# Redistributing the eight PSUM banks of a recurrence: three for projections, two for values, outputs and norms, three shared by levels, key transposes and state increments

## The chip, the cores and the metric

The kernel runs on one core of one Trainium2 chip. The metric is the device time of one execution in microseconds (us); where several runs are shown, their median stands.

## What is computed

One trunk layer of a hybrid diffusion model over 128 context and 1024 latent tokens (1152 in all, D_MODEL 1024): a gated feed-forward half step, a token mixer, and a second feed-forward half step. The mixer projects the normalised input with `w_in` and splits the result; one part goes to attention, the other to a gated recurrence (HGRN2, 8 heads of 64, run forward and backward). The change lies in the recurrence:

```python
def hgrn2_chunked(q, k, logf, v, s0):
    ...
    A = jnp.einsum('bntshk,bnthk,bnshk->bnhts', decay, qc, kc)
    o_intra = jnp.einsum('bnhts,bnshv->bnthv', A, vc)
    g = b[:, :, -1]
    dS = jnp.einsum('bnshk,bnshv->bnhkv', kc * jnp.exp(g[:, :, None] - b), vc)
    def step(S, inp):
        gj, dSj = inp
        return jnp.exp(gj)[..., None] * S + dSj, S
    s_final, S_prev = lax.scan(step, s0.astype(jnp.float32), ...)
    o_inter = jnp.einsum('bnthk,bnhkv->bnthv', qc * jnp.exp(b), S_prev)
    return (o_intra + o_inter).reshape(B, T, H, DV), s_final
...
    q_h = jax.nn.silu(heads(hq, HG_DK))
    f_fw = lb_h[0] + (1.0 - lb_h[0]) * jax.nn.sigmoid(heads(hf_f, HG_DK))
    o_rec = rmsnorm(o_fw + flip(o_bw), hg_norm_g) * jax.nn.silu(heads(hgate, HG_DV))
```

## The kernel before

One program on one core: first feed-forward, mixer (recurrence, attention, merge), second feed-forward. Activations lie features on partitions, tokens along the free dimension. The 1152 tokens are cut into three chunks of CW = 384, worked in ORDER (2, 0, 1); the 8 heads go in 4 pairs, and a 128-partition tile holds a head's forward state in its lower and its backward state in its upper half.

**Projections.** One projection of one chunk is 8 blocks of 128 inputs, each with three float32r products (high times high L467, low times high L468, high times low L469), so 24 matmuls that add up in one PSUM bank of tag `mm`. `dense_g` yields after the first 12, so that other work of the weave can come between the halves. Readers of the bank: `proj_f` (forget gate: ACT sigmoid L664, then L676), `proj_q` (sigmoid L664, DVE multiply L687), `proj_v` (ACT copy `t` L698), `proj_gate` (sigmoid L664, DVE multiply L742, then POOL's multiply L735 with the normed output), `proj_sg` (sigmoid L664, then a DMA). Weights come by SP's queue and are split into a high part on ACT (`wh`, L230 or L240) and a low part (`wl`, DVE L233 or POOL L241).

**Recurrence.** `scan_pre` makes, of one head and chunk, the cumulated gates: `kk` (ACT L867, L868), a copy of q (L871), X and Y (ACT L877, DVE L879 to L882, POOL), then the scaled keys and queries `Kb`, `Qb`, `KE` (DVE L887 to L900). `scan_lev` takes them through the levels: matmuls of keys and queries within blocks of 8, then 16, 32, 64 tokens (`lv`, L932), each level read by DVE (copy_predicated L939, L974) or ACT (L958), with DVE's decays of KE (L969) and ACT's copies of its halves (`kr`, L944 and L945) in between; then it turns the keys (`kt`, L984, copied by ACT L986), and multiplies them with the values into the chunk's state increments (`dS`, L994, copied by ACT L995). `scan_out` runs the states (DVE L1004) and adds inter and intra parts up in PSUM (`po`), which ACT copies out (L1020). `turn_v` turns the projected values (`vt`, L705, ACT copy L706). After a pair's two heads, `proj_gate` squares the output, and its inner `norm` calls `rec_norm` for the three chunks: a matmul with ones (`ops`), then ACT and DVE (L359 to L363), then L1030. The norm before the mixer does the same with `nps` (L451, in `stat_end`), its tag given by `self.st`.

**Banks.** The PSUM pool `pp` of this stage has all 8 banks of 512 floats: `lv` 3, `sm` 3, `mm` 2 (L759 to L761). A tile takes the banks of its tag in turn, and its first matmul waits until the last reader of the bank's former tile is done. Before, `sm` holds `nps`, `vt`, `kt`, the increments (`dS`), `po` and `ops`. `attn`, which follows, has a pool of its own over the same eight banks, with three `mm` banks.

**Order.** Every engine runs its instructions in one fixed order. `hgrn` weaves projections, the current chunk's levels (`cur`), the former chunk's end (`old`), the next one's `scan_pre` (`pre`) and the outputs by hand, in groups and slots; the framework's scheduler then places each instruction when the program is built, by what it takes to be ready, and so the number of banks can move instructions on each engine. A few are pinned in program order.

Of the kernel before, what the change touches and what calls it, by code (L numbers as in the profile page):

```python
# [9 lines left out]
F32 = mybir.dt.float32  # L10
# [9 lines left out]
P = 128  # L20
# [6 lines left out]
CW = 384  # L27
# [3 lines left out]
ORDER = (2, 0, 1)  # L31
# [57 lines left out]
class Trunk:  # L89
# [550 lines left out]
    def mixer(self):  # L640
        nc, tc = self.nc, self.tc
        dram = lambda n, sh: self.dp.tile(sh, F32, name=n)
        self.sg = dram("sgates", [2, KT, P, T])
        self.orec = dram("orec", [4, P, T])
        self.oat = dram("oat", [4, P, T])
        with ExitStack() as st:
            self.fp = st.enter_context(tc.tile_pool(name="hp", bufs=1, reuse_waits="tile"))
            self.pp = st.enter_context(tc.tile_pool(name="pp", bufs=1, space=PSUM, reuse_waits="tile"))
            self.st, self.nt, self.hfb = ("sm", 3), ("t", 3), 2
            self.hgrn()  # L650
        with ExitStack() as st:
            self.kp = self.fp = st.enter_context(tc.tile_pool(name="kp", bufs=1, reuse_waits="tile"))
            self.pp = st.enter_context(tc.tile_pool(name="pp", bufs=1, space=PSUM, reuse_waits="tile"))
            self.attn()
# [45 lines left out]
            yield  # L700

    def turn_v(self, out, c, t):
        pt = self.pp.tile([P, CW], F32, tag="sm", bufs=3, name="vt")
        for j in range(3):
            self.nc.tensor.transpose(pt[:, ts(j, P)], t[:, ts(j, P)], self.ident)  # L705
        self.nc.scalar.copy(out["V"][:, c * CW : (c + 1) * CW], pt)  # L706
        out["nv"] = out.get("nv", 0) + 1
# [48 lines left out]

    def hgrn(self):
        nc, pin = self.nc, self.tc.keep_in_program_order
        self.mmb = 2  # L759
        for tag, n in (("lv", 3), ("sm", 3), ("mm", 2)):  # L760
            self.pp.tile([P, 512], F32, tag=tag, bufs=n, name=tag)  # L761
        f32 = lambda n, sh: self.fp.tile(sh, F32, name=n)
        A, B = slice(0, 64), slice(64, P)
        self.kr = {m: f32(f"kr{m}", [P, CW]) for m in (8, 16, 32, 64)}
        self.XY = [f32(n, [P, 48, 8]) for n in "XY"]
        self.A1 = [f32(f"A1_{i}", [P, 3, G]) for i in range(2)]
        self.A2 = f32("A2", [P, 3, G])
        self.cnt, self.later = 0, []
        heads = [{} for _ in range(H)]
        pairs = [{} for _ in range(4)]  # L770
        sgs = [self.proj_sg(j) for j in range(2 * KT)]

        def feed(h):
            p = h // 2
            r = [self.proj_f(5 * p + h % 2, h, heads[h])]
            if h % 2 == 0:
                r += [self.proj_q(5 * p + 2, pairs[p]), self.proj_v(5 * p + 3, pairs[p])]
            return r

        def scan_of(h):  # L780
            p = h // 2
            if h % 2 == 0:
                pairs[p]["o"] = self.tt(F32, "oT")
            d = heads[h]
            d["pair"] = pairs[p]
            d["h"], d["QP"], d["As"] = h, self.tt(F32, "QP"), {}
            d["Gall"] = self.fp.tile([P, 9], F32, tag="Gall", bufs=2, name="Gall")
            return d

        def work_of(h):  # L790
            p = h // 2
            work = feed(h + 1) if h + 1 < H else []
            if h and h % 2 == 0:
                work = work + [sgs.pop(), sgs.pop()] + [self.proj_gate(5 * p - 1, p - 1, pairs[p - 1])]
            while len(work) < 4 - (h == 3) + (h == H - 1):
                work.append(sgs.pop())
            return chain(*work)

        pre = iter(())
        for i, _ in enumerate(weave(feed(0))):  # L800
            if i < 12:
                next(self.tail, None)
            if i == 11:
                assert next(self.tail, 1)
                for t in self.XY:
                    pin(nc.vector.memset(t[:, :, 3:4], 1.0))
                d = scan_of(0)
                pre = self.scan_pre(d, ORDER[0])
            if i == 13:
                for t in self.A1 + [self.A2] + list(self.kr.values()):  # L810
                    pin(nc.vector.memset(t, 0.0))
            next(pre, None)
        for _ in pre:
            pass
        self.group()
        work = chain.from_iterable(map(work_of, range(H)))
        old = cur = out = last = None
        for p in range(H * NCH + 1):
            h, n = divmod(p, NCH)
            old, cur, pre = cur, None, iter(())  # L820
            if h < H:
                cur = self.scan_lev(d, ORDER[n])
            if p + 1 < H * NCH:
                h1, n1 = divmod(p + 1, NCH)
                while min(heads[h1].get("nf", 0), pairs[h1 // 2].get("nq", 0)) <= n1:
                    next(work)
                if n1 == 0:
                    last, d = d, scan_of(h1)
                pre = self.scan_pre(d, ORDER[n1])

            def slots(k):
                for _ in range(k):
                    next(work, None)
                    next(pre, None)

            self.group(old, cur)
            slots(3)
            self.group(old, cur, old, out)
            slots(2 + p % 2)
            self.group(cur, out, old)  # L840
            out = None
            if p and n == 0:
                out = self.scan_out(last if h < H else d)
                next(out)
            slots(2)
            for _ in pre:
                pass
        self.group(out, out)
        for _ in work:
            pass  # L850
        for n, _ in enumerate(self.proj_gate(19, 3, pairs[3])):
            if n == 0:
                self.group()
# [51 lines left out]
    def scan_lev(self, d, b):  # L905
# [10 lines left out]
        dS = d["dS"]  # L916
# [6 lines left out]
        lv = lambda: self.pp.tile([P, 3, 64], F32, tag="lv", bufs=3, name="lv")  # L923
# [25 lines left out]
        for li, m in enumerate((8, 16, 32, 64)):  # L949
# [29 lines left out]
                    nc.scalar.copy(Af[u, :, u], Ad[u])  # L979
            Tm = Tn  # L980
            yield
        pt = self.pp.tile([P, 3, P], F32, tag="sm", bufs=3, name="kt")
        for j in range(3):
            nc.tensor.transpose(pt[:, j], KE[:, ts(j, P)], self.ident)  # L984
        kT = tmp("kT", 2, (P, 3, P))
# [1 line left out]
        yield  # L987
        V = d["pair"]["V"]
        assert d["pair"]["nv"] > ORDER.index(b)
        pd = self.pp.tile([P, 3, 64], F32, tag="sm", bufs=3, name="dS")  # L990
        for j in range(3):
            for r in (A, B):
                v = V[:, (3 * b + j) * P + 64 * hh : (3 * b + j) * P + 64 * hh + 64]
# [3 lines left out]
    def scan_out(self, d):  # L997
        nc = self.nc
        h, V, QP, Gall, S, dS = d["h"], d["pair"]["V"], d["QP"], d["Gall"], d["S"], d["dS"]
        A, B = slice(0, 64), slice(64, P)  # L1000
        nc.sync.dma_start(self.o["st"][h], dS[:, 8])
        for j in range(7):
            for r, s0, s1, g in ((A, j, j + 1, j), (B, 7 - j, 6 - j, 7 - j)):
                nc.vector.scalar_tensor_tensor(S[r, s1], S[r, s0], Gall[r, g : g + 1], dS[r, g], ALU.mult, ALU.add)  # L1004
        yield
        off = 64 * (h % 2)
        r = slice(off, off + 64)
        for pairs, lows, highs in (((3, 4), (2, 5)), (2, 4), (4, 6)), (((1, 6), (0, 7), (8,)), (0, 2), (6, 9)):
            po = self.pp.tile([P, 3, P], F32, tag="sm", bufs=3, name="po")
            at = lambda t: po[A, t - lows[0]] if t < lows[1] else po[B, t - highs[0]]  # L1010
            for pair in pairs:
                for t in pair:
                    w = V[:, t * P + off : t * P + off + 64]
                    nc.tensor.matmul(at(t), w, d["As"][t // 3][:, t % 3], start=True, stop=(t == 8))
                for t in pair:
                    if t < 8:
                        nc.tensor.matmul(at(t), S[:, t], QP[:, ts(t, P)], start=False, stop=True)
            for half, (t0, t1) in ((A, lows), (B, highs)):
                pv = po[half, : t1 - t0].rearrange("p a b -> p (a b)")
                nc.scalar.copy(d["pair"]["o"][r, t0 * P : t1 * P], pv)  # L1020
            d["pair"]["no"] = d["pair"].get("no", 0) + 1
            yield

    def rec_norm(self, c, oT, sq):
        nc = self.nc
        cs = slice(c * CW, (c + 1) * CW)
        ps = self.pp.tile([P, CW], F32, tag="sm", bufs=3, name="ops")
        nc.tensor.matmul(ps, self.onesb, sq[:, cs], start=True, stop=True)
        self.rstd(sq[:, cs], ps)
        nc.vector.scalar_tensor_tensor(oT[:, cs], oT[:, cs], self.hg, sq[:, cs], ALU.mult, ALU.mult)  # L1030
# [873 lines left out]
```

## Time and profile before

| what | value |
|---|---|
| median of 3 runs | 2897.6 us (2895.7 to 2897.98) |
| profiled execution, its own time | 2896.19 us |
| its span | 2894.2 us |
| mean granted TensorE clock | 0.989 |
| instructions in the span | 54329 |

The span runs from the first to the last recorded instruction; the 2 us around it belong to the execution's time. Engines: PE is TensorE's matmuls, PEld its weight loads, DVE VectorE, ACT ScalarE, POOL GpSimd, SP the engine that issues DMAs. In a timeline row stand start, duration, engine, source line, operation, result and operands, shape, and in brackets the idle time of the engine just ahead of it with what released it. The recurrence stretches from about 838 us (its norm `nps`) to 1431 us, where attention's first projection starts.

### The profile page before, as it was taken

How to read it: one execution, taken by the hardware profiler on the slowest of the kernel's cores; microseconds unless marked ns; L12 is line 12 of the kernel's file. 1: busy time of each engine (PE TensorE's matmuls, PEld its weight loads, DVE VectorE, ACT ScalarE, POOL GpSimd, SP SyncE). 2: the span in 40 equal slices, each digit the busy share in tenths (PEclk: the TensorE clock that was granted, in tenths of full speed). 3: DMA queues.
4: the chain of work that ended last, by engine and by line, in shares of the span. 5: the costliest groups of instructions: out<-in, count | busy, mean ns of one | idle time of the engine just before them, and what ended most of it. 6: DMA issues, size and time to landing. Idle time of an engine off the chain costs nothing. (4 is left out here: it accounts for less than half of the span.)

```text
span 2894.2 us, 54329 instructions
## 1 busy us (share of the span) xinstructions
PE 2803.6 (97%) x20946; PEld 2665.0 (92%) x20946; DVE 1967.4 (68%) x4292; ACT 1278.4 (44%) x2566; POOL 943.4 (33%) x896
## 2 busy tenths in 40 slices
PE   6999999999999999999998999899999999999998
PEld 5999999999999988888987777699999999999997
DVE  7687777577778787876266777856756665556665
ACT  6433222321166677766446777711642323333102
POOL 0133332454222222222145454433333232236321
PEclk9999999999999999999998999999999999999999
DMA  6643333653121111112100001333442322235211
GB/s 240 212 146 119 131 116 122 234 192 117 56 74 65 45 56 39 56 46 74 68 17 17 13 16 49 100 126 101 166 133 95 105 83 77 73 134 186 91 46 66
DMA packets 151490, 282.43 MB, mean 98 GB/s; under 512 B 19200, under 2 KB 83776, under 8 KB 151232
## 3 DMA queue, kind: packets, MB, share of 16 engines
q1 hardware_dynamic: 151232, 278.96, 28.0%
q8 instruction: 165, 2.70, 0.4%
q14 instruction: 93, 0.76, 0.1%
HBM read 215.37 MB, written 63.52 MB: 96 GB/s over the span
## 5 line engine op out<-in xcount | busy, mean ns | idle before, releaser
L1652 PE MATMUL b<-xo,wo 128*128 128x288 f32 x3552 | 482.4, 295 | 0.0
L1652 PEld LDWEIGHTS b<-xo,wo 128*128 128x128 f32 x3552 | 474.5, 188 | 0.0
L496 DVE SCALAR_TENSOR_TENSOR x<-dn,modt,x 128x256 f32<-128x256 f32 (+4 forms) x728 | 353.4, 505 | 168.8 <-PE dn L469 166.2
L1652 PE MATMUL b<-bh,wo 128*128 128x288 f32 x1776 | 365.9, 295 | 1.2 <-ACT et L1662 1.2
L467 PE MATMUL mm<-xh,wh 128*128 128x384 f32 (+1 forms) x1008 | 352.1, 349 | 10.8 <-DVE sg L742 6.0
L468 PE MATMUL mm<-xl,wh 128*128 128x384 f32 (+1 forms) x1008 | 342.1, 339 | 0.0
L469 PE MATMUL mm<-xh,wl 128*128 128x384 f32 (+1 forms) x1008 | 341.4, 339 | 0.0
L1652 PEld LDWEIGHTS b<-bh,wo 128*128 128x128 f32 x1776 | 289.2, 188 | 1.5 <-ACT et L1662 1.4
L1652 PE MATMUL b<-bl,wo 128*128 128x288 f32 x888 | 262.4, 295 | 0.0
L241 POOL TENSOR_TENSOR wl<-raw,wh 128x1024 fp32r<-128x1024 f32 (+3 forms) x71 | 151.3, 2133 | 273.4 <-ACT wh L240 270.7
L1627 ACT CAST wo<-raw 128x512 fp32r<-128x512 f32 x185 | 114.7, 621 | 227.6 <-PE b L1652 117.4
L467 PEld LDWEIGHTS mm<-xh,wh 128*128 128x128 f32 (+1 forms) x1008 | 189.6, 188 | 20.9 <-DVE sg L742 8.2
L467 PE MATMUL dn<-hh,wh 128*128 128x384 f32 (+2 forms) x576 | 196.7, 341 | 1.7 <-DVE et L1668 0.9
L1628 DVE TENSOR_TENSOR wo<-raw,wo 128x512 fp32r<-128x512 f32 x185 | 127.2, 688 | 103.3 <-ACT wo L1627 100.4
L469 PE MATMUL dn<-hh,wl 128*128 128x384 f32 (+2 forms) x576 | 194.4, 337 | 1.0 <-POOL wl L241 1.0
L468 PE MATMUL dn<-hl,wh 128*128 128x384 f32 (+2 forms) x576 | 194.6, 338 | 0.0
L468 PEld LDWEIGHTS mm<-xl,wh 128*128 128x128 f32 (+1 forms) x1008 | 189.4, 188 | 2.3 <-issue 0.7
L469 PEld LDWEIGHTS mm<-xh,wl 128*128 128x128 f32 (+1 forms) x1008 | 189.3, 188 | 1.0
L1730 POOL TENSOR_TENSOR hl<-hr,hh 128x1152 fp32r<-128x1152 f32 x44 | 118.0, 2689 | 193.8 <-ACT hh L1729 92.5
L312 DVE SCALAR_TENSOR_TENSOR junk<-wada,cb 128x512 bf16<-128x512 f32 x224 | 165.7, 740 | 8.5 <-DMA wada<-in_w_aT 7.8
L1384 POOL TENSOR_TENSOR ehl<-e,ehl 128x512 fp32r<-128x512 f32 x93 | 122.5, 1322 | 142.1 <-ACT ehl L1382 79.0
L1652 PEld LDWEIGHTS b<-bl,wo 128*128 128x128 f32 x888 | 167.2, 188 | 0.0
(392 smaller groups left out, 6867.8 us busy)
## 6 DMA issues: line engine op xcount, KB each, us to landing
raw<-in_w SPq DMA_DIRECT2D x148, 256.0 KB, 3.2
raw<-in_w SPq DMA_DIRECT2D x58, 512.0 KB, 3.7
wada<-in_w_aT SPq DMA_DIRECT2D x112, 256.0 KB, 2.9
hr<-hs SPq DMA_DIRECT2D x44, 576.0 KB, 5.2
hs<-et SPq DMA_DIRECT2D x148, 144.0 KB, 1.8
raw<-in_w_in SPq DMA_DIRECT2D x41, 512.0 KB, 3.2
hb<-hd SPq DMA_DIRECT2D x44, 288.0 KB, 3.4
x<-in_xT SPq DMA_DIRECT2D x16, 576.0 KB, 6.4
```

Source lines behind the costliest of these rows:

```text
L241: pin((eng or self.nc.gpsimd).tensor_sub(wl, raw, wh))
L312: nc.vector.scalar_tensor_tensor(junk, ws[n % 2], 1.0, cs[s], ALU.mult, ALU.mult, accum_out=o)
L467: pin(nc.tensor.matmul(ps, wh, xh, start=start and i == 0, stop=False))
L468: pin(nc.tensor.matmul(ps, wh, xl, start=False, stop=False))
L469: pin(nc.tensor.matmul(ps, wl, xh, start=False, stop=stop and i == n - 1))
L496: nc.vector.scalar_tensor_tensor(self.x[m][:, a:b], ps[:, a - lo : b - lo], self.modt[:, gm, m, s : s + 1], self.x[m][:, a:b], ALU.mult, A ...
L1384: eng.tensor_sub(el, e, eh)
L1627: nc.scalar.copy(wh, src[i])
L1628: nc.vector.tensor_sub(wl, src[i], wh)
L1652: nc.tensor.matmul(ps, w[:, k], x[:, k, :QW], start=first, stop=last, skip_group_check=home != i)
L1730: nc.gpsimd.tensor_sub(hl, raw, hh)
```

## The change

Eight banks stay eight. `mm` has three and `sm` two. `nps`, `kt` and the increments move from `sm` to `lv`; `vt` and `po` stay in `sm`; of the three `ops` of a pair the first two stay in `sm`, and the third takes an `mm` bank.

```diff
--- before.py
+++ after.py
@@ -646,7 +646,7 @@
         with ExitStack() as st:
             self.fp = st.enter_context(tc.tile_pool(name="hp", bufs=1, reuse_waits="tile"))
             self.pp = st.enter_context(tc.tile_pool(name="pp", bufs=1, space=PSUM, reuse_waits="tile"))
-            self.st, self.nt, self.hfb = ("sm", 3), ("t", 3), 2
+            self.st, self.nt, self.hfb = ("lv", 3), ("t", 3), 2
             self.hgrn()
         with ExitStack() as st:
             self.kp = self.fp = st.enter_context(tc.tile_pool(name="kp", bufs=1, reuse_waits="tile"))
@@ -700,7 +700,7 @@
             yield
 
     def turn_v(self, out, c, t):
-        pt = self.pp.tile([P, CW], F32, tag="sm", bufs=3, name="vt")
+        pt = self.pp.tile([P, CW], F32, tag="sm", bufs=2, name="vt")
         for j in range(3):
             self.nc.tensor.transpose(pt[:, ts(j, P)], t[:, ts(j, P)], self.ident)
         self.nc.scalar.copy(out["V"][:, c * CW : (c + 1) * CW], pt)
@@ -756,8 +756,8 @@
 
     def hgrn(self):
         nc, pin = self.nc, self.tc.keep_in_program_order
-        self.mmb = 2
-        for tag, n in (("lv", 3), ("sm", 3), ("mm", 2)):
+        self.mmb = 3
+        for tag, n in (("lv", 3), ("sm", 2), ("mm", 3)):
             self.pp.tile([P, 512], F32, tag=tag, bufs=n, name=tag)
         f32 = lambda n, sh: self.fp.tile(sh, F32, name=n)
         A, B = slice(0, 64), slice(64, P)
@@ -979,7 +979,7 @@
                     nc.scalar.copy(Af[u, :, u], Ad[u])
             Tm = Tn
             yield
-        pt = self.pp.tile([P, 3, P], F32, tag="sm", bufs=3, name="kt")
+        pt = self.pp.tile([P, 3, P], F32, tag="lv", bufs=3, name="kt")
         for j in range(3):
             nc.tensor.transpose(pt[:, j], KE[:, ts(j, P)], self.ident)
         kT = tmp("kT", 2, (P, 3, P))
@@ -987,7 +987,7 @@
         yield
         V = d["pair"]["V"]
         assert d["pair"]["nv"] > ORDER.index(b)
-        pd = self.pp.tile([P, 3, 64], F32, tag="sm", bufs=3, name="dS")
+        pd = self.pp.tile([P, 3, 64], F32, tag="lv", bufs=3, name="dS")
         for j in range(3):
             for r in (A, B):
                 v = V[:, (3 * b + j) * P + 64 * hh : (3 * b + j) * P + 64 * hh + 64]
@@ -1006,7 +1006,7 @@
         off = 64 * (h % 2)
         r = slice(off, off + 64)
         for pairs, lows, highs in (((3, 4), (2, 5)), (2, 4), (4, 6)), (((1, 6), (0, 7), (8,)), (0, 2), (6, 9)):
-            po = self.pp.tile([P, 3, P], F32, tag="sm", bufs=3, name="po")
+            po = self.pp.tile([P, 3, P], F32, tag="sm", bufs=2, name="po")
             at = lambda t: po[A, t - lows[0]] if t < lows[1] else po[B, t - highs[0]]
             for pair in pairs:
                 for t in pair:
@@ -1024,7 +1024,8 @@
     def rec_norm(self, c, oT, sq):
         nc = self.nc
         cs = slice(c * CW, (c + 1) * CW)
-        ps = self.pp.tile([P, CW], F32, tag="sm", bufs=3, name="ops")
+        tag = ("sm", 2) if ORDER.index(c) < 2 else ("mm", 3)
+        ps = self.pp.tile([P, CW], F32, tag=tag[0], bufs=tag[1], name="ops")
         nc.tensor.matmul(ps, self.onesb, sq[:, cs], start=True, stop=True)
         self.rstd(sq[:, cs], ps)
         nc.vector.scalar_tensor_tensor(oT[:, cs], oT[:, cs], self.hg, sq[:, cs], ALU.mult, ALU.mult)
```

One line is added, so lines behind L1027 have a number higher by one in the changed kernel.

In the built program the numbers of instructions and SP's order stay as they were. Orders differ on PE, DVE, ACT and POOL at the start of the recurrence only, in the stretch from about 845 to 905 us of the profile before. On PE, the third projection of each round of the first feed (f, q, v) now runs its first 12 matmuls ahead of the second halves of the other two, and the third chunk's value transposes (`vt`) stand 10 rows earlier among the level products.

On ACT, before the change, from the sigmoid of the third forget projection of head 0 (`sg_9356`) on, to the key copies of the first chunk and the first value copy. `kr32` and `kr64` are the key halves of levels 32 and 64, `kk`, `X`, `Y` belong to the `scan_pre` of head 0's third chunk, `wh` are weights of the projections to come, `t` and `V` the turned values:

```order
L664 ACTIVATE sg_9356<-mm_9282 128x384
L676 ACTIVATE fs_9035<-sg_9356,lb_86,lb1_87 64x384 x2
L867 ACTIVATE kk_9718<-fs_9035 64x384
L868 ACTIVATE kk_9718<-fs_9035 64x384
L877 COPY X_9030<-fs_9035 128x48
L877 COPY Y_9031<-fs_9035 128x48
L230 COPY wh_9629<-raw_9627 128x1024
L664 ACTIVATE sg_9382<-mm_9303 128x384
L945 COPY kr32_9028<-KE_9339 64x6x32
L944 COPY kr64_9029<-KE_9339 64x3x64
L230 COPY wh_9850<-raw_9848 128x1024
L698 COPY t_9397<-mm_9324 128x384
```

On ACT at the same place after the change:

```order
L664 ACTIVATE sg_9356<-mm_9282 128x384
L945 COPY kr32_9028<-KE_9339 64x6x32
L676 ACTIVATE fs_9035<-sg_9356,lb_86,lb1_87 64x384 x2
L664 ACTIVATE sg_9382<-mm_9303 128x384
L230 COPY wh_9629<-raw_9627 128x1024
L944 COPY kr64_9029<-KE_9339 64x3x64
L698 COPY t_9397<-mm_9324 128x384
L706 COPY V_9092<-vt_9399 128x384
L706 COPY V_9092<-vt_9404 128x384
L945 COPY kr64_9029<-KE_9339 64x3x64
L706 COPY V_9092<-vt_9409 128x384
L867 ACTIVATE kk_9718<-fs_9035 64x384
```

The key copy L945 of `kr32` now stands right behind the sigmoid and ahead of the pair L676 of the forget gate; `kk`, `X` and `Y` and the weights `wh_9850` have gone behind the value copies.

On DVE, at the same place in the program, before the change, from the second keys of head 0 (`Kb_9553`) to the state of the first chunk's keys (`KE_9339`, which L945 reads) and the third q multiply. `wl` is the low part of the weights:

```order
L887 TENSOR_TENSOR Kb_9553<-kk_9471,Y_9031 64x384
L233 TENSOR_TENSOR wl_9454<-raw_9451,wh_9453 128x512 x2
L888 TENSOR_TENSOR Qb_9554<-qx_9474,X_9030 64x384
L892 COPY TK_9573<-Y_9031 64x48
L893 COPY TK_9573<-X_9030 64x48
L894 TENSOR_TENSOR TQ_9574<-X_9030,fs_9035 64x48
L895 TENSOR_TENSOR TQ_9574<-Y_9031,fs_9035 64x48
L900 TENSOR_TENSOR KE_9555<-Kb_9553,TK_9573 128x384
L896 TENSOR_TENSOR T8_9575<-TK_9573,TQ_9574 128x48
L969 TENSOR_TENSOR KE_9339<-KE_9339,T16_9528 64x12x16
L969 TENSOR_TENSOR KE_9339<-KE_9339,T32_9596 64x6x32
L879 TENSOR_TENSOR X_9030<-fs_9035,X_9030 128x48
```

On DVE at the same place after the change:

```order
L887 TENSOR_TENSOR Kb_9553<-kk_9471,Y_9031 64x384
L888 TENSOR_TENSOR Qb_9554<-qx_9474,X_9030 64x384
L892 COPY TK_9573<-Y_9031 64x48
L893 COPY TK_9573<-X_9030 64x48
L894 TENSOR_TENSOR TQ_9574<-X_9030,fs_9035 64x48
L895 TENSOR_TENSOR TQ_9574<-Y_9031,fs_9035 64x48
L900 TENSOR_TENSOR KE_9555<-Kb_9553,TK_9573 128x384
L896 TENSOR_TENSOR T8_9575<-TK_9573,TQ_9574 128x48
L969 TENSOR_TENSOR KE_9339<-KE_9339,T16_9528 64x12x16
L969 TENSOR_TENSOR KE_9339<-KE_9339,T32_9596 64x6x32
L233 TENSOR_TENSOR wl_9454<-raw_9451,wh_9453 128x512 x2
L969 TENSOR_TENSOR KE_9339<-KE_9339,T32_9596 64x6x32
```

The pair L233 of `wl_9454` has moved from ahead of the keys' scaling to behind the L969 multiplies of `KE_9339`.

The third place is on PE near the end of the third pair, at about 1237 us of the profile before, where the order stays and only the waits differ. `mm_14459` is a forget projection, `lv_14475` a level product of the older chunk, `lv_14501` and `lv_14502` the first products of the next chunk, forward and backward half; in brackets stand the engines whose semaphores an instruction waits for. Before the change:

```order
L469 MATMUL mm_14459<-xh3_8452,wl_14455 128x384
L932 MATMUL lv_14475<-QP_13551,kr32_9028 32x32 [waits DVE_49,Pool_49]
L932 MATMUL lv_14475<-QP_13551,kr32_9028 32x32 x11
L932 MATMUL lv_14501<-Qb_14359,Kb_14358 32x32
L932 MATMUL lv_14502<-Qb_14359,Kb_14358 32x32 [waits DVE_49,PE_49]
```

After the change:

```order
L469 MATMUL mm_14459<-xh3_8452,wl_14455 128x384
L932 MATMUL lv_14475<-QP_13551,kr32_9028 32x32 [waits DVE_49,Pool_49]
L932 MATMUL lv_14475<-QP_13551,kr32_9028 32x32 x11
L932 MATMUL lv_14501<-Qb_14359,Kb_14358 32x32 [waits DVE_49,PE_49]
L932 MATMUL lv_14502<-Qb_14359,Kb_14358 32x32 [waits Activation_49]
```

The bank of `lv_14502` was last read by DVE before the change; now its last reader is ACT, whose copy L995 takes the increments of an earlier chunk out of that bank.

Behind the recurrence, attention's first projection keeps its place. Its bank was last read by the third norm's readers before, and by the L742 multiply of the last gate projection after.

## The prediction

> **What bounds the kernel now.** I read the page's engine table first, then the windows view over the recurrence (the only place the change touches), then the waits of PE there, and last single rows of the timeline.
>
> ```profile
> span 2894.2 us, 54329 instructions
> PE 2803.6 (97%) x20946; PEld 2665.0 (92%) x20946; DVE 1967.4 (68%) x4292; ACT 1278.4 (44%) x2566; POOL 943.4 (33%) x896
> ```
>
> Over the whole span PE is the bound: 2803.6 of 2894.2 us. But this share is a mean over stages. The next fence cuts the recurrence into stretches; the columns are the stretch, its length, and the busy time of PE, weight load, DVE, ACT and POOL, then the granted clock.
>
> ```profile
> 838.00:883.00 45.00, 43.01 (x265) 41.30 (x265) 36.32 (x79) 31.42 (x64) 9.69 (x15) 0.94 0.14 48
> 883.00:950.00 67.00, 67.00 (x779) 63.40 (x778) 54.20 (x151) 41.84 (x107) 15.02 (x26) 0.97 0.22 75
> 1015.00:1248.00 233.00, 223.63 (x2737) 205.82 (x2730) 189.93 (x497) 168.90 (x404) 53.66 (x91) 0.99 0.14 50
> 1337.00:1417.00 80.00, 80.00 (x823) 75.70 (x823) 27.29 (x76) 35.48 (x85) 12.93 (x15) 1.00 0.22 78
> 1431.00:1510.00 79.00, 79.00 (x445) 74.81 (x444) 40.85 (x64) 27.36 (x48) 34.47 (x29) 1.00 0.08 26
> ```
>
> In 883 to 950, 1337 to 1417 and 1431 to 1510 PE never stops: whatever delays PE there delays the end. In 1015 to 1248 it stands still for 233.00 - 223.63 = 9.4 us. What PE waits for, over the whole recurrence up to 1431 (total, times, longest):
>
> ```profile
> PE mm L467 <- DVE sg L742: 6.0, 5, 1.8
> PE mm L467 <- DVE q L687: 4.3, 3, 2.3
> PE mm L467 <- ACT sg L664: 0.4, 1, 0.4
> ```
>
> These are the waits of a projection's first matmul for a bank: 6.0 + 4.3 + 0.4 = 10.7 us, 0.37% of the time, and all that a third bank could give back.
>
> Who drives the middle stretch decides what those waits are worth. I followed the work back from the last copy below to the first row below, each time to what released an instruction or to the instruction ahead of it on its engine.
>
> ```profile
> 1015.01 0.49 ACT L664 ACTIVATE sg<-mm 128x384 f32<-128x384 f32 x1 [1.89 <-issue]
> 1247.70 0.47 ACT L698 COPY t<-mm 128x384 f32<-128x384 f32 x1
> 1248.23 0.55 PE L705 MATMUL vt<-ident,t 128*128 128x128 f32 x3 [0.65 <-ACT t L698]
> ```
>
> Between these two ACT rows lie 530 instructions end to end (330 of DVE, 191 of ACT, 9 of POOL), none of PE, with no stop but table loads and hand-overs. PE enters at 1015 and takes over again at 1248.23, where it waits 0.65 us for ACT. The two engines wait for each other inside the stretch, not for PE:
>
> ```profile
> ACT Af L979 <- DVE Ad L977: 20.6, 8, 3.8
> ACT kk L867 <- DVE Kb L887: 17.1, 8, 3.9
> ...
> DVE X L879 <- ACT X L877: 8.2, 5, 2.0
> DVE S L1004 <- ACT dS L995: 7.9, 5, 2.3
> ```
>
> So from 1015 to 1248 the length is set by the ACT and DVE chain, and PE's waits there are its slack.
>
> **The change, part by part.** Counts of instructions, SBUF addresses and DMA issues stay the same, and the order on SP too. On PE, DVE, ACT and POOL the order differs only at the start of the recurrence, about 845 to 905 us; behind it only PE's bank waits differ.
>
> *Third projection bank.* The built program no longer waits at these first matmuls:
>
> ```profile
> 849.98 0.45 PE L467 MATMUL mm<-xh,wh 128*128 128x384 f32 x1 [0.40 <-ACT sg L664]
> 1078.22 0.44 PE L467 MATMUL mm<-xh,wh 128*128 128x384 f32 x1 [0.48 <-DVE sg L742]
> 1114.72 0.44 PE L467 MATMUL mm<-xh,wh 128*128 128x384 f32 x1 [2.32 <-DVE q L687]
> 1336.76 0.44 PE L467 MATMUL mm<-xh,wh 128*128 128x384 f32 x1 [0.47 <-DVE sg L742]
> ```
>
> With the two other q L687 waits that makes 0.40 + 0.48 + 4.3 + 0.47 = 5.65 us. The three remaining waits for L742, 6.0 - 0.48 - 0.47 = 5.05 us, stay: the third norm (`ops` of the last chunk) now takes the third bank, so the next projection still stands behind the first gate's multiply. Of the 5.65 us, the 0.48 and the 4.3 lie inside the chain stretch, where I cost them at **0**; if that cover were gone they would be worth -4.78. The 0.47 at 1336.76 stands right ahead of a stretch in which PE is never idle: **-0.47**. The 0.40 belongs to the start, below.
>
> *Key transposes, increments and the first norm in the level banks.* Now a level product can meet a bank whose reader is ACT's copy of the transposes (L986) or of the increment (L995). By the rows of before, five products would come too early; these are the largest three, each with the copy that it now waits for:
>
> ```profile
> 980.10 0.62 PE L932 MATMUL lv<-Qb,Kb 64*32 64x32 f32 x48
> 980.30 0.32 ACT L995 COPY dS<-dS 128x192 f32<-128x192 f32 x1
> ...
> 1107.39 0.62 PE L932 MATMUL lv<-Qb,Kb 64*32 64x32 f32 x48
> 1107.86 0.32 ACT L995 COPY dS<-dS 128x192 f32<-128x192 f32 x1
> ...
> 1237.68 0.62 PE L932 MATMUL lv<-Qb,Kb 64*32 64x32 f32 x48
> 1238.84 0.32 ACT L995 COPY dS<-dS 128x192 f32<-128x192 f32 x1
> ```
>
> The copies end at 980.62, 1108.18 and 1239.16: waits of 0.52, 0.79 and 1.48 us, 2.79 together, and two more that are each shorter than the first, at most 1.04: 3.83 at the outside. Behind the waiting product stand, on PE, the remaining products of that level and the next projection half; DVE waits for the products, ACT's sigmoid for the projection. What hides it: at 1237.68 the next projection's bank would have come late in before, and the copy at 1247.70 reads a projection that PE finished ahead of this row:
>
> ```profile
> 1245.88 0.89 PE L932 MATMUL lv<-QP,kr 128*64 128x64 f32 x36
> ```
>
> That is a lead of 1247.70 - 1245.88 = 1.8 us against a delay of 1.48 at most, and freed q L687 waits lie between. I take **0**; the bound above is 3.83, the one below 0, since a wait added on PE frees nothing.
>
> *The start.* With three banks the third projection of a round runs its first half ahead of the first two's second halves, and ACT's and DVE's orders follow. PE does the same matmuls. What stands on the path is ACT ahead of the value transposes:
>
> ```profile
> 874.29 0.48 ACT L664 ACTIVATE sg<-mm 128x384 f32<-128x384 f32 x1
> 874.81 1.44 ACT L676 ACTIVATE fs<-sg,lb,lb 64x384 f32<-64x384 f32 x2
> ...
> 880.53 0.35 ACT L945 COPY kr<-KE 64x192 f32<-64x192 f32 x1 [1.05 <-DVE KE L969]
> 881.00 0.35 ACT L944 COPY kr<-KE 64x192 f32<-64x192 f32 x1
> 881.25 1.04 ACT L230 CAST wh<-raw 128x1024 fp32r<-128x1024 f32 x1
> 882.20 0.47 ACT L698 COPY t<-mm 128x384 f32<-128x384 f32 x1
> ...
> 875.75 1.29 DVE L233 TENSOR_TENSOR wl<-raw,wh 128x512 fp32r<-128x512 f32 x2
> 880.02 0.94 DVE L969 TENSOR_TENSOR KE<-KE,T 64x192 f32<-64x192 f32 x2
> ```
>
> The key copy L945 moves ahead of L676, directly behind the sigmoid that ends at 874.77. DVE's weight pair of 1.29 us moves behind the key multiplies, so the copy starts at 880.53 - 1.29 = 879.24; then 0.35, L676 1.44, the next sigmoid 0.48, the weight cast 1.04, a key copy 0.35: t is copied at 882.90 in place of 882.20, **+0.70**. The kk, X and Y of the chunk after (L867, L877) fall behind the value copies, by some 6 us; PE's 67.00 of 67.00 us behind 883 hides that, since it works on projections. From below, the freed 0.40 at 849.98 bounds it: -0.40. From above, see the third rival.
>
> A rule on the clock belongs beside these stalls. Behind the 2.32 us stall the trace has this:
>
> ```profile
> 1116.20:1119.60 3.40, 3.40 (x46) 2.78 (x44) 3.27 (x8) 1.80 (x3) 0.88 (x1) 0.50 0.02 5
> ```
>
> So a stall can cost a further 3.4 us at 0.50 of the clock, 1.7 us of work, and this one lies inside the chain stretch. The Trainium skill, "TensorE: Matmul & The Clock Gate", section "What's actually happening", says that the clock is halved after at least one idle window of about 3.4 us, that the window runs free and that the same kernel can meet it at another phase. The length agrees with the row; the stall here was shorter than the window, so the measurement is the stricter one. By the page the waits added here, all below 1.7 us, would halve no clock and the sum would stay as it is; by the row a halved window more or less is possible in any run.
>
> *The tail.* Attention's first projection keeps its place, but its bank is now that of the last gate's last projection:
>
> ```profile
> 1430.80 0.34 PE L467 MATMUL mm<-xh,wh 128*128 128x384 f32 x1
> 1431.92 0.56 DVE L742 TENSOR_TENSOR sg<-mm,sg 128x384 f32<-128x384 f32 x1 [1.34 <-POOL sg L735]
> ```
>
> PE started it without a wait at 1430.80; now it waits for DVE's multiply, which ends at 1432.48: **+1.68**. Behind it on PE stands all of attention's projecting, 79.00 of 79.00 us busy, so nothing hides it. A halved window behind it would add 1.7.
>
> **Sum** on the profiled execution of 2896.19 us (span 2894.2): 0 - 0.47 + 0 + 0.70 + 1.68 = +1.91. That execution lies 1.41 below the median of three, 2897.6; the same step on the median gives **2899.5 us**.
>
> **Rivals.**
>
> *A, PE is the bound after all.* For it: 97% busy. The Trainium skill, "Perfetto Trace Analysis", section "Optimization Strategy", takes a repeated gap on the engine that should be saturated as a sign of too little PSUM; by it this change is the remedy. As a mechanism of this kernel: all 5.65 us freed count, the tail's 1.68 stays, ACT's copies come earlier with PE so that the level waits cost nothing: 2897.6 - 5.65 + 1.68 = 2893.6, and 2891.9 if the halved window at 1116 goes too. Against it: the unbroken 530 steps without PE.
>
> *B, the level waits are passed on.* If PE's lead of 1.8 us before ACT is used up, the 3.83 us count: 2899.5 + 3.83 = 2903.3. It decides from a delay beyond 1.8 us; the largest here is 1.48, and a halved window of 1.7 behind it would go past that.
>
> *C, the start stalls ACT (slower).* If DVE's multiply for L945 does not come 1.29 us earlier, and the work behind it (L676, casts, sigmoid) is needed sooner than I count, ACT stands from 874.77 to 880.53, 5.76 us, and all of it reaches the transposes: 2899.5 - 0.70 + 5.76 = 2904.6. It decides once L676's result, now after 879.6 and not 874.81, is what the next stage waits for. For it: a wait put ahead of ready work in an in-order queue. Against it: ACT's 31.42 busy of 45 us leaves room to catch up.
>
> *D, the change does less than it says.* Since the third norm takes the bank, half of the removed waits stay anyway; this is in the sum already.
>
> **How the numbers follow.** Forecast 0.65 (2895.5 to 2902.5: the start's -0.40, a halved window more or less, the spread of the runs shown), A 0.14, B 0.08, C 0.13. About 0.2%, 5.8 us, is what a measurement of this kernel can tell from no change. Faster than 2891.8 needs A with the halved window and some more: 0.08, of A. Slower than 2903.4 takes C, half of B and a little of the forecast with a halved window: 0.18. The rest, 0.74, is within. The range reaches to A's lower end and C's time: 2892 to 2905.
>
> **What would show it.** Right: the first matmuls at 1114.72, 1235 and 1241 without waits, yet the copy of t before the transposes at 1248 as long after the sigmoid at 1015 as before (232.7 us); waits of PE for ACT's dS copy at about three places; a wait of 1.7 us before attention's first projection, named L742. Wrong: the distance from 1015 to 1248 shrinking by over 2 us (A), or growing by over 2 us (B), or ACT idle for over 5 us before L945 at about 875 with PE idle behind it (C). A halved window that appears in one and not in the other kernel would shift the time by 1.7 us for no reason of the change.

## The result, and the profile after

The changed kernel takes 2904.59 us (median of 9 runs, 2900.89 to 2905.91), the kernel before 2896.7 us (9 runs, 2895.1 to 2897.98): a ratio of 1.0025, 95% interval 1.0016 to 1.0034. It is slower by 7.9 us, where 1.9 us was forecast; the time lies just inside the upper end of the range (2905), 2.1 us above the band of the forecast itself (2895.5 to 2902.5).

Head of the page after:

```profile
span 2902.8 us, 54343 instructions
PE 2805.7 (97%) x20946; PEld 2669.4 (92%) x20946; DVE 1966.0 (68%) x4292; ACT 1278.5 (44%) x2566; POOL 940.7 (32%) x896
```

No engine has more work than before (PE's 2.1 us more go with a clock that is halved for 73.6 us of the span instead of 66.8): the span has grown by waits and by halved clock. The waits of PE over the recurrence of the changed kernel (total, times, longest):

```profile
PE mm L467 <- DVE sg L742: 6.6, 4, 1.8
PE vt L705 <- ACT V L706: 5.0, 1, 5.0
PE nps L451 <- DVE rs L377: 4.5, 1, 4.5
PE lv L932 <- ACT dS L995: 3.4, 3, 2.3
PE vt L705 <- ACT t L698: 2.6, 4, 1.6
PE lv L932 <- DVE QP L969: 1.9, 2, 1.6
PE lv L932 <- POOL QP L969: 1.3, 1, 1.3
PE dS L994 <- ACT kT L986: 0.8, 1, 0.8
```

The bank waits for q L687 are gone, as the change promises, and so are two of the five for L742; one for L742 is new, ahead of attention. Three rows are new: a single wait of 5.0 us of the value transposes for ACT, 3.4 us of level products for ACT's copies of the increments, and one of 1.3 us of level products for POOL.

**A ledger.** One and the same matmul (the n-th of its source line) can be looked up in two traces. The table gives, by stage, how much later than in the profile of before the matmuls start at the stage's end, less the same at its beginning; each end is the middle value of the matmuls in 1.2 us of before's time. "Ahead" is what an execution had lost before the recurrence began, which the change cannot touch. The last column but one is the sum of the five stages from 839 to 1431.

| stage (us of before) | ahead | 839-905 | 905-1015 | 1015-1249 | 1249-1337 | 1337-1431 | recurrence | 1431-2870 |
|---|---|---|---|---|---|---|---|---|
| changed kernel | 1.41 | 3.43 | 0.25 | 1.29 | 0.91 | 1.87 | 7.75 | -0.57 |
| the same again (e8) | 0.77 | 3.60 | 0.17 | 0.17 | -0.66 | 1.84 | 5.12 | 2.29 |
| e1 levels only | 1.18 | 0.04 | 0.11 | 0.08 | 0.12 | 0.03 | 0.38 | 1.61 |
| e2 start restored | 0.40 | -0.35 | 0.22 | -0.21 | -0.65 | 0.04 | -0.95 | 2.76 |
| e3 tail restored | -0.22 | 3.21 | 0.26 | 0.27 | -0.64 | -0.12 | 2.98 | 2.35 |
| e4 start and tail | 1.56 | -0.84 | 0.18 | 0.29 | -0.66 | -0.05 | -1.08 | 1.24 |
| e5 before again | -0.28 | 0.08 | 0.01 | 0.10 | 0.01 | 0.03 | 0.23 | -0.53 |

The two executions of the changed kernel agree on three entries: the start, 3.4 to 3.6 us; the last pair's freed wait and what follows, when no halved window falls there; and the tail, 1.8 us. They differ by 1.1 and 1.6 us in 1015-1249 and 1249-1337, and behind the recurrence.

**The start.** ACT's rows in the changed kernel, where the chain to the value transposes runs; then DVE's and PE's:

```profile
877.07 0.48 ACT L664 ACTIVATE sg<-mm 128x384 f32<-128x384 f32 x1
881.92 0.35 ACT L945 COPY kr<-KE 64x192 f32<-64x192 f32 x1 [4.37 <-DVE KE L969]
882.30 1.44 ACT L676 ACTIVATE fs<-sg,lb,lb 64x384 f32<-64x384 f32 x2
883.76 0.49 ACT L664 ACTIVATE sg<-mm 128x384 f32<-128x384 f32 x1
884.27 1.04 ACT L230 CAST wh<-raw 128x1024 fp32r<-128x1024 f32 x1
885.23 0.35 ACT L944 COPY kr<-KE 64x192 f32<-64x192 f32 x1
885.48 0.47 ACT L698 COPY t<-mm 128x384 f32<-128x384 f32 x1
885.85 0.85 ACT L706 COPY V<-vt 128x384 f32<-128x384 f32 x2
...
881.54 0.74 DVE L969 TENSOR_TENSOR KE<-KE,T 64x192 f32<-64x192 f32 x2
882.20 1.28 DVE L233 TENSOR_TENSOR wl<-raw,wh 128x512 fp32r<-128x512 f32 x2
...
886.37 0.90 PE L705 MATMUL vt<-ident,t 128*128 128x128 f32 x3 [4.98 <-ACT V L706]
```

ACT stands 4.37 us in front of the key copy L945, and everything behind it in its queue waits along. In before it did L676 and other work in that time, and waited 1.05 us for the same copy. Less the 1.41 us of "ahead", L945 starts at 880.51; in before it was 880.53. So it did not come earlier at all, though the weight pair L233 has indeed gone behind DVE's key multiply. The reason lies further up, from the first sigmoid of the stage on:

```profile
851.01 0.62 ACT L402 ACTIVATE xh<-xn,modt 128x384 fp32r<-128x384 f32 x1 [1.50 <-DVE xn L401]
851.65 1.28 ACT L664 ACT_TABLE_LOAD   x1
852.95 0.49 ACT L664 ACTIVATE sg<-mm 128x384 f32<-128x384 f32 x1
...
855.46 0.56 DVE L687 TENSOR_TENSOR q<-mm,sg 128x384 f32<-128x384 f32 x1 [3.17 <-ACT sg L664]
...
865.53 1.60 DVE L811 MEMSET kr<- 128x384 f32 x4
...
869.29 0.55 DVE L887 TENSOR_TENSOR Kb<-kk,X 64x384 f32<-64x384 f32 x1
```

The same rows of before:

```profile
848.14 1.28 ACT L664 ACT_TABLE_LOAD   x1
849.43 0.49 ACT L664 ACTIVATE sg<-mm 128x384 f32<-128x384 f32 x1
849.82 0.61 ACT L402 ACTIVATE xh<-xn,modt 128x384 fp32r<-128x384 f32 x1
...
852.30 0.56 DVE L687 TENSOR_TENSOR q<-mm,sg 128x384 f32<-128x384 f32 x1 [1.22 <-ACT sg L664]
...
866.32 0.55 DVE L887 TENSOR_TENSOR Kb<-kk,X 64x384 f32<-64x384 f32 x1
...
882.72 0.55 PE L705 MATMUL vt<-ident,t 128*128 128x128 f32 x3 [1.59 <-ACT t L698]
```

In the new order ACT does the fourth L402 ahead of its table load, and waits 1.50 us for DVE's norm to do it; the first sigmoid comes 852.95 - 849.43 - 1.41 = 2.1 us later. DVE waits 3.17 us for ACT's sigmoids in place of 1.22, and stands idle for 5.3 us in all between its fourth L401 and its first scaled keys, in before for 4.0; these keys come 869.29 - 866.32 - 1.41 = 1.56 us later. That eats the 1.29 us that the weight pair was to give back. The transposes start 886.37 - 882.72 - 1.41 = 2.24 us late. Some 0.4 us of this come from the two banks of values and outputs: t is copied by 885.95, but the third value tile then waits for ACT's copy L706 of the first one to free its bank, hence the name of the wait; in before it waited for t alone. The other 1.2 us of the stage lie behind the transposes, where the clock stays halved for two windows (885.6 to 892.5); before it was one (884.1 to 887.5).

**The clock.** Two stretches of 3.4 us in the changed kernel, and what follows each (columns as in the windows view: stretch, length, PE, weight load, DVE, ACT, POOL, granted clock, DMA share, GB/s):

```profile
1134.80:1138.20 3.40, 1.81 (x77) 1.17 (x76) 2.75 (x11) 3.10 (x8) 0.55 (x1) 1.00 0.02 5
1138.20:1141.60 3.40, 3.40 (x12) 3.40 (x13) 3.19 (x10) 1.88 (x7) 0.03 (x1) 0.50 0.00 0
1336.20:1339.60 3.40, 1.61 (x10) 1.38 (x9) 1.96 (x5) 3.34 (x5) 1.27 (x2) 1.00 0.02 5
1339.60:1343.00 3.40, 3.40 (x13) 3.40 (x12) 3.24 (x7) 3.30 (x8) 0.68 (x2) 0.50 0.16 58
```

And in before, ahead of its halved window at 1116, and at a stall that brought none:

```profile
1112.80:1116.20 3.40, 1.48 (x8) 1.48 (x9) 3.25 (x10) 1.03 (x2) 0.00 (x0) 1.00 0.00 0
1328.00:1331.50 3.50, 2.00 (x43) 1.40 (x42) 3.34 (x8) 3.44 (x5) 0.00 (x0) 1.00 0.00 0
```

Three of these four windows at full clock, with PE busy for 44 to 53% of them, were followed by one at 0.50; the one with 57% was not. Before, the halved window fell at 1116, inside the stretch where PE has slack, and cost nothing: e1 below has none there, and takes as long for this stretch (232.8 us against 232.7). In the first profile of the changed kernel halved windows fell at 1138 and 1339.6, and cost 1.3 and 1.6 us, the second right ahead of a stretch in which PE never idles. In its second profile three such windows (1079, 1130, 1243) lay in PE's slack, and 1015-1249 grew by 0.17 us only. That is the difference between the two rows of the ledger from 1015 to 1337.

**The tail.** PE's first projection of attention, and the multiply it waits for, in the changed kernel:

```profile
1439.86 0.44 PE L467 MATMUL mm<-xh,wh 128*128 128x384 f32 x1 [1.57 <-DVE sg L742]
...
1439.25 0.56 DVE L742 TENSOR_TENSOR sg<-mm,sg 128x384 f32<-128x384 f32 x1 [1.33 <-POOL sg L735]
```

In before PE had no wait there. In the ledger 1337-1431 grows by 1.87 and 1.84.

### The profile page after: what moved, and what is told of

It reads as the page before. It is cut to its first block, busy times and chain, and to the rows that moved or that the text cites. A ratio compares the mean times of both kernels' runs of the same rounds, so it can differ in the third digit from the quotient of the medians.

```text
span 2902.8 us, 54343 instructions
## 1 busy us (share of the span) xinstructions
PE 2805.7 (97%) x20946; PEld 2669.4 (92%) x20946; DVE 1966.0 (68%) x4292; ACT 1278.5 (44%) x2566; POOL 940.7 (32%) x896
```

## The experiments

Theory L, formed from these traces: the level waits lie in PE's slack, the freed bank waits of the middle too, and the loss is the start's new order, the tail, and halved windows in costlier places. Its main rival is B of the prediction, that the level waits are passed on.

**e1, levels only.** On the kernel before:

```diff
-        pt = self.pp.tile([P, 3, P], F32, tag="sm", bufs=3, name="kt")
+        pt = self.pp.tile([P, 3, P], F32, tag="lv", bufs=3, name="kt")
...
-        pd = self.pp.tile([P, 3, 64], F32, tag="sm", bufs=3, name="dS")
+        pd = self.pp.tile([P, 3, 64], F32, tag="lv", bufs=3, name="dS")
```

> The kernel before, with nothing changed but the banks of the key transposes and the state increments, which share the levels' three (three stay for values, outputs and norms, two for projections). Every engine's order is that of before. Theory L (the ledger: the level waits lie in PE's slack, the loss comes from the start of the recurrence, from halved clock windows and from the tail): 0, within 1 us of before. Theory B (the waits of level products for ACT's copies are passed on): 2.5 to 3.8 us slower than before. In the trace both expect PE waits at L932 for L995, 3 us or so in all.

2899.81 us against 2896.95: 1.0008, interval 1.0 to 1.0017. In its profile the level products wait as forecast:

```profile
PE lv L932 <- ACT dS L995: 2.2, 3, 1.3
```

yet the recurrence grows by 0.38 us in the ledger: B is out there. The time alone would not say so: it is 2.9 us longer by the medians, which misses theory L's 1 us and falls into B's range. What it shows beyond the recurrence is lost behind 2102 us, at the opening of the second feed-forward; more on it below.

**e2, start restored**, and **e4, start and tail restored**, on the changed kernel. The first holds a projection bank until the first feed is through:

```diff
+        hold = self.pp.tile([P, CW], F32, tag="mm", bufs=3, name="hold")
+        pin(nc.tensor.matmul(hold[:, :8], self.ones, self.ones[:, :8], start=True, stop=True))
...
         self.group()
+        pin(nc.vector.tensor_copy(self.fp.tile([P, 8], F32, name="freed"), hold[:, :8]))
         work = chain.from_iterable(map(work_of, range(H)))
```

> The changed kernel, but with one projection bank held back until the first feed is through (one matmul of 8 columns and one small copy more), so that the start of the recurrence runs in the order of before, all but the third value transpose. Theory L: the start cost 3.4 us, so 3 to 3.5 us faster than the changed kernel, 4 to 5 us slower than before; ACT's wait for L945 of 4.4 us near 878 is gone. Theory B: the start is worth the 0.7 us that was forecast, so about 7 us slower than before.

2899.17 us against 2896.95: 1.0012 (1.0004 to 1.0021). The start's 3.4 us are gone (-0.35 in the ledger). So is the tail's wait (0.04), which this run was to keep: the bank held back turned the rotation of the projection banks, so that, by the order of the tiles, attention's first projection got the third norm's bank as in before; its wait for L742 is gone. So e2 undoes both, which fits that it came out faster than expected. e4 adds the edit of e3:

> Both of these edits on the changed kernel. Theory L: 3.4 + 1.7 us off the changed kernel's 7.9, so 2 to 3.5 us slower than before, what is left being halved clock windows in new places. Theory B: 5.5 us slower than before, what is left being the level waits. If the third projection bank were worth anything by itself, it would show here: faster than before.

2899.48 us: 1.0014 (1.0005 to 1.0023), as expected, and no gain from a third bank. Its recurrence is 1.08 us shorter than before's in the profile; its time is longer all the same.

**e3, tail restored**, on the changed kernel (with `p` handed down to `rec_norm`):

```diff
-        tag = ("sm", 2) if ORDER.index(c) < 2 else ("mm", 3)
+        tag = ("sm", 2) if p == 3 or ORDER.index(c) < 2 else ("mm", 3)
```

> The changed kernel, but the third norm of the last pair takes a bank of the values and outputs and not one of the projections, so that attention's first projection gets a bank that is free. Theory L: 1.7 us faster than the changed kernel, about 6.2 us slower than before; the wait of some 1.7 us for L742 ahead of attention's first projection is gone. Rival: the third norm's wait for its bank takes its place, then as slow as the changed kernel, 7.9 us slower than before.

2901.89 us: 1.0021 (1.0013 to 1.003), some 5 us above before. The ledger has -0.12 in 1337-1431 against 1.87 and 1.84: the wait was worth what the rows of before said. The start is there again (3.21).

**e5 and e8, both kernels once more.**

> The kernel before, unchanged but for a comment at its end. Every theory expects the time of before; how far the median of its runs lies from that of before says what a difference of this size is worth, and its profile gives a second set of halved clock windows for one and the same program.

> The changed kernel, unchanged but for a comment at its end: 2901 to 2906 us. A second profile: theory L expects the start again 3 to 3.5 us longer and the tail 1.7 us, and the halved windows near 1138 and 1339 of the first profile elsewhere or absent, since their places hang on the phase.

Before: 2896.43 against 2896.7, 1.0 (0.9991 to 1.0009), with halved windows within 0.5 us of their places in the first profile. So 0.1% is what these comparisons can tell. Changed: 2904.22 us, 1.0027 (1.0016 to 1.0038), with the ledger above.

**e6, start alone.** The bank is held from behind the first feed to the end of the recurrence, and `rec_norm` takes `tag = ("sm", 2)` for all three norms.

> The changed kernel, with three projection banks for the first feed alone: behind it one bank is held back until the recurrence ends (one matmul of 8 columns and one small copy more), and all three norms use the banks of values and outputs. So the start's new order is there, two projection banks afterwards, and no wait ahead of attention's first projection. Theory L: the start costs 3.2 to 3.5 us in the profile between the norm near 838 and 905 us, and the time is 3 to 4 us above before. Theory B or a gain of the third bank elsewhere: a start that costs 0.7 us and a time of before or 1 to 4 us above it without a loss near 880.

2904.14 us: 1.0027 (1.0017 to 1.0038). The start costs 3.38 us, as expected, and 905-1249 nothing (-0.33). The rest of the expectation fell: the norms in two banks wait, with a halved window behind the last of these waits at 1332, and 1249-1337 grows by 1.9 us; and attention's first projection got the held bank and waited 1.64 us for its release. So this run bears out the start by its stage, not by its time.

**e7, all waits freed.** e2 with all three norms in `sm`.

> The start restored as in the run e2, and all three norms of each pair in the banks of values and outputs, so that projections have three banks to themselves: the waits of the second gate projection for L742 near 1073, 1331 and 1426, some 5 us, are gone too. Theory L (the chain of ACT and DVE sets the stretch from 1015 to 1248): the distance from ACT's sigmoid near 1015 to the copy ahead of the transposes near 1248 stays within 0.5 us of before's 232.7; only the waits near 1331 and 1426 come back, 1 to 3 us, so 1 to 4 us faster than e2. Rival A (PE is the bound): that distance shrinks by 3 us or more.

2903.98 us: 1.0023 (1.0013 to 1.0032), not faster than e2 but 3 to 5 us slower (by the ratios, by the medians). The bank waits of the projections behind the first feed are gone, and this stands in their place from 1015 to 1345 in its profile:

```profile
PE ops L1032 <- DVE rt L361: 8.3, 3, 3.0
```

The third norm's matmul, with two banks, waits for DVE to read the first norm, 3 us at a time, and PE's queue behind it; halved windows follow (1134.7, 1243.9, 1332.6), and 1015-1249 grows by 3.4 us, 1249-1337 by 2.0. Theory L's 1 to 4 us did not come. Neither did rival A's.

**e9, more instructions**, on the kernel before: seven matmuls of 8 columns on PE that nobody reads, at the start of `hgrn`.

> The kernel before with seven matmuls of 8 columns more on PE at the start of the recurrence, whose result nobody reads; banks and orders are those of before. They stand for the 14 or so instructions more that the changed kernels have in their records. Theory I (a longer instruction stream or a later start of what follows moves the second feed-forward's opening): 1.5 to 3 us slower than before, with the loss between 2100 and 2200 us in the profile. Theory N (it does not, and the 2 us that the run e1 shows belong to the banks): within 0.7 us of before, and no loss between 2100 and 2200.

2899.27 against 2895.88 us: 1.0013 (1.0004 to 1.0022). In its profile 3.0 us are lost at 838 us already, where the matmuls stand and the clock stays halved for 10.2 us in place of 6.8 (half of it is made up by 905), and nothing to speak of from 2100 to 2200 (0.07). So it does not bear out theory I; its time, which misses N's 0.7 us for this other reason, says nothing on N.

**e10, three banks only**: e4 with `kt` and the increments back in `sm`, now with `bufs=2`.

> The run e4 (start and tail restored) with key transposes and state increments back in the two banks of values and outputs, so that the levels have their three to themselves and only the third projection bank is left of the change. Theory L: the level waits cost nothing, and the transposes and increments lose nothing in two banks: as e4, 2 to 3.5 us slower than before. Theory B: 2 to 4 us faster than e4, at or below the time of before. Rival: waits of transposes and increments for ACT's copies in two banks take their place, 2 us or more slower than e4.

2903.73 against 2895.88 us: 1.0026 (1.0014 to 1.0039), 3.5 us worse than e4 by the ratios, though the two intervals overlap. The rival of that expectation holds in its profile:

```profile
PE vt L705 <- ACT kT L989: 6.2, 2, 4.1
```

The longer of the two waits, 4.1 us, stands at the value transposes behind 1248, where PE takes over. Two banks for values, outputs, transposes and increments are too few; with three banks for projections, the sharing of the levels' banks is what keeps the loss small. From 1015 to 1248, where this kernel has the freed waits and no level wait for an increment, it takes as long as before (232.6 us): there the freed waits by themselves bring nothing.

**e11 and e12, second profiles of e1 and e4**, one run each.

> The kernel of run e1 once more, for a second profile. If the 1.5 us that e1 lost at the opening of the second feed-forward (2102 to 2200 us) belong to the program, they are there again; if they belong to the single execution, the opening is as in before, within 0.3 us. The recurrence is again within 0.5 us of before.

> The kernel of run e4 once more, for a second profile. If the loss of 1.3 us behind 2102 us belongs to the program, it is there again. The recurrence is again about 1.5 us shorter than in before unless a halved clock window falls where PE is never idle, which would make it 1.7 us longer.

e11 loses 1.4 us behind 2102 us again (e1: 1.7). Its recurrence is 0.4 us shorter than before's in all, with a loss of 0.9 us at a halved window near 1336 included. e12 loses 1.2 us there again (e4: 1.3). Its recurrence is 2.2 us longer than before's, not shorter: a clock halved for 6.8 us from 1238.7, after which the value copy of t at 1249.30 waits 0.88 us for PE, and one halved window more at 1334.

**The distance that decides between chain and PE**, from ACT's sigmoid near 1015 to the copy of t near 1248 (start to start; 1020.10 and 1254.09 in the changed kernel):

| kernel | us |
|---|---|
| before, e5 | 232.7, 232.8 |
| changed, e8 | 234.0, 232.3 |
| e1, e11 (levels share, two projection banks) | 232.8, 232.1 |
| e2, e3, e4, e12 (bank waits freed) | 232.5, 232.3, 232.5, 233.4 |
| e6, e9, e10 | 232.2, 232.2, 232.6 |
| e7 (norms in two banks) | 235.2 |

Three projection banks or two, level waits or none: it stays within 0.6 us of before's, apart from three executions in which halved windows (the changed kernel's first profile, e12) or the norm's waits (e7) held PE past its lead.

**What stays open.** DVE's first steps of the second feed-forward wait for a spill to memory to land. The wait in before, and then in e1, where the instructions there are the same and in the same order:

```profile
DVE xn L406 <- DMA hd<-xn: 5.4, 2, 3.3
```

```profile
DVE xn L406 <- DMA hd<-xn: 7.0, 2, 4.8
```

The longest wait is 3.3 us in both profiles of before and 3.5 in e9, but 4.2 to 5.0 in all eleven profiles with other banks. It belongs to the program, then, and costs 1.2 to 1.7 us where the ledger has been split there (e1, e4, e8, e11, e12). In e1 the two weight loads of 512 KB issued around the spill took longer too, 4.5 us in the median from issue to landing against 3.6 in before. Why, isn't shown: e1's program differs from before's by PSUM banks in the recurrence and by 15 more semaphore instructions on PE, and by nothing else; e9, longer by seven matmuls, does not show it.

## Why the prediction was right or wrong

- **The middle: right.** PE's bank waits do not set 1015 to 1248. The freed waits of 4.8 us brought nothing there (e2, e4, e8, and e10 without level waits), and the level waits (3.4 us, forecast at 3.83 at the outside) cost nothing (e1). Rival A is out: with PE as the bound the distance above would have shrunk by some 4.8 us in the changed kernel, and it shrank by 0.4 in e8. The Trainium skill, "Perfetto Trace Analysis", section "Optimization Strategy", says that a repeated gap on the engine that should be saturated can mean too little PSUM; in this stretch it did not. One step of the argument was too strong, though. "The two engines wait for each other inside the stretch, not for PE" leaves out rows of the same two views, and the walk from row to row meets PE between the two ACT rows, at a weight copy:

```profile
ACT kr L944 <- PE lv L932: 3.8, 3, 1.8
...
DVE QP L969 <- PE lv L932: 3.8, 3, 3.0
...
1164.65 1.05 ACT L230 CAST wh<-raw 128x1024 fp32r<-128x1024 f32 x1 [0.36 <-PE mm L468]
```

  So the walk does run through PE there, if only by 0.36 us. That PE's bank waits are slack is shown by the runs, not by the walk.
- **The waits that stay, the last pair, the tail: right.** Three L742 waits stayed; the freed one at 1336.76 brought some 0.65 us for the 0.47 forecast; the tail took 1.84 to 1.87 for 1.68, and nothing hid it.
- **The start: the failed step.** "DVE's weight pair of 1.29 us moves behind the key multiplies, so the copy starts 880.53 - 1.29 = 879.24." It started where it had. I followed the new order from the sigmoid of the third chunk on, and took what stands ahead of it as unmoved; but ACT's and DVE's orders differ from the first L402 on, and those rows cost DVE 1.56 us. The term was sized at 0.70 and measured 3.4 to 3.6; in the first profile 2.24 of it lie on the path to the transposes and 1.2 behind them, at a halved clock. This is rival C's place and mechanism, ACT standing behind a wait put ahead of ready work (4.37 us, short of the 5 us that the prediction had named as C's sign), at 60% of its price.
- **The clock: mechanism seen, place missed.** The prediction allowed a window more or less "for no reason of the change". Part of it has a reason: where a freed wait lets PE run ahead, idle time gathers at the next place where PE waits for ACT, and a halved window can follow there (1138 and 1339.6 in the first profile of the changed kernel, against 1116 in before). Part of it has none in the program: the two profiles of the changed kernel differ by it by 1.1 us in 1015-1249 and by 1.6 us in 1249-1337.
- **Outside the recurrence: not forecast.** 1.2 to 1.7 us at the second feed-forward's opening.
- **The sum.** Forecast 0 - 0.47 + 0 + 0.70 + 1.68 = 1.91. Measured in e8: 0.17 + 0.17 at 905-1249, -0.66, 3.60, 1.84, and 2.29 behind: 7.41, against 7.5 to 7.9 us in the times. The first profile comes to about the same, 7.75 - 0.57 = 7.18, by other parts. The range held because it reached up to rival C's time. That the measured time equals C's 2904.6 is luck: C had 5.76 us at the start and nothing outside the recurrence, where the start took 3.4 to 3.6 and e8 lost 2.3 us behind it.

No version beat the kernel before. e1, without a third projection bank, came nearest (1.0008); with three banks it was e2 and e4 (1.0012 and 1.0014).

## What to carry to other kernels

A gap on an engine that is 97% busy is worth nothing where other engines' work sets the length of the stretch: follow the chain back before pricing the gap, and test it by a run that changes the gaps alone. A change of buffer counts can reorder every engine at the place where buffers first run out; walk the new order there from its first differing row, because an in-order engine that meets a wait early holds up all ready work behind it. And no bank was free here: giving one to the projections made another tenant wait, the norms (e7), the transposes (e10) or attention (the change itself).

## What the runs showed of the hardware

The granted clock goes by windows of 3.41 us on a fixed grid. Over the fourteen profiles, between 990 and 1440 us, every window at full clock with PE busy for 43% or less (ten of them) was followed by one at half clock, none with more than 56% was, and in between it went either way (worked out from the matmul rows, whose ends are modelled). So some 2 us of waiting within one window were always enough, and whether two waits of 1 us share a window decides as much as their length. The Trainium skill, "TensorE: Matmul & The Clock Gate", section "What's actually happening", names a whole idle window as the condition; the windows shown above, with 1.5 to 1.8 us of work in them, were not idle, and the measurement decides.
